# A two-layer diffusion block on one core: modulation rows loaded in half blocks and moved out of the second layer's FFN, FFN parts chosen by layer, input sums on VectorE

## The chip, the cores and the metric

One core of a Trainium2 chip runs the whole program. The metric is device time in microseconds for one execution.

## The reference

Two layers run over 128 prompt tokens and 512 sample tokens, width 1024, float32. Two condition vectors, one for the prompt and one for the sample, give each layer a modulation of 6 × 1024 values:

```python
mod = silu(cond) @ w_ada[l] + b_ada[l]
sh1, sc1, g1, sh2, sc2, g2 = split(mod, 6)
h = rmsnorm(x, norm1_g) * (1 + sc1) + sh1
x = x + g1 * mixers(h)               # retention, differential and latent attention, gated, projected
h = rmsnorm(x, norm2_g) * (1 + sc2) + sh2
a, b = split(h @ w_ffn_in, 2)        # 1024 -> 2 x 2816
x = x + g2 * ((silu(a) * b) @ w_ffn_out)
```

After both layers a last RMSNorm gives the outputs; the mixers also return their caches.

## The kernel before

**Layout.** Activations lie transposed: 128 channels on the partitions, the 640 tokens along the free axis in two halves of 320. Each float32 product is made of three matmuls of `hi`/`lo` pairs, so every weight block is loaded as `raw`, cast by ScalarE to `whi` (L117), and VectorE subtracts to give `wlo` (L120). Layer 0 is called the first layer here, layer 1 the second.

**Modulation rows.** A layer's 6144 modulation values are 48 rows of 128 channels. `ada_rows` (L237) makes a row: POOL issues the load of a 128x1024 block `rawr` (L245), and VectorE multiplies it with each of the two conditions and sums into one column of `mod` (L248, two instructions a row, held in program order on VectorE). After the last row of a call it adds the bias to all rows of the call (L252). Rows 0 to 15 are sh1 and sc1, 16 to 23 g1, 24 to 39 sh2 and sc2, 40 to 47 g2.

**When rows are made.** `plan` gives each row a due point, `fill` is called at points in the stage, and rows that are due are issued there; what is left is issued by `flush`. Rows 16 to 39 are planned over the last branch and the output projection, which have 20 points; `norm2` for the first half flushes the rest. Rows 40 to 47 are planned at the very start of the layer's FFN (share 0 to 0.0277 of 72 points), with one `rawr` tile. In the first layer's FFN rows 0 to 15 of the second layer follow at shares 0.15 to 0.9.

**FFN** (`ffn`, L1217). The 22 blocks f of 128 hidden channels go through `up`: blocks 0 to NC-1 (NC = 5) in the plain form of 96 matmuls, the rest through `ffn_seven` (L1177), seven products and 84 matmuls, which needs sums of input quarters made by `ffn_forms` (L1120) from the eight `us` tiles. These sums run on POOL (L1130 to L1133). The results are the tiles `ghi`/`glo`, GB = 6 of each, which the `us` tiles share until the sums are made. The down projection goes in seven parts (FFN_PARTS): a part's eight units n each load weights (L1286) and for both halves multiply into a PSUM tile G or O and add the gated result to `x` (`x_add`, L1073). `x_add` reads g2, that is rows 40 to 47 with their bias. There are two such PSUM tiles, so a third down product waits for the first `x_add`. The units of a part are issued three after each `up` of the next part.

**Order.** The tile framework orders each engine's instructions by a timeline it works out when the program is built; only pinned instructions (the row products, and matmuls after block NC) keep their order in the program. Engines run their queues in order, so a VectorE instruction that waits for a load holds what is queued behind it.

Of the kernel before, what the change touches and what calls it, by code (L numbers as in the profile page):

```python
# [12 lines left out]
F32 = mybir.dt.float32  # L13
# [8 lines left out]
P = 128  # L22
# [15 lines left out]
FFN_PARTS = ((0, 3), (3, 6), (6, 9), (9, 12), (12, 15), (15, 18), (18, 22))  # L38
GB = 6
NC = 5  # L40
# [10 lines left out]
class Kern:  # L51
# [185 lines left out]
    def ada_rows(self, l, b0, b1, pool, raws, bufs):  # L237

        d = self.dve
        if l not in self.mod:  # L240
            self.mod[l] = self.const.tile([P, 48, 2], F32, name=f"mod{l}")
        mod = self.mod[l]
        for n in range(b0, b1):
            raw = raws.tile([P, 1024], F32, tag="rawr", name="rawr", bufs=bufs)
            self.pool.dma_start(out=raw, in_=self.io["w_adat"][l, n])  # L245
            junk = pool.tile([P, 1024], mybir.dt.bfloat16, tag="junk", name="junk")
            for i in range(2):
                self.tc.keep_in_program_order(d.scalar_tensor_tensor(  # L248
                    junk, raw, 1.0, self.csr[:, i, :], op0=ALU.mult, op1=ALU.mult, accum_out=mod[:, n, i:i + 1]))
            if n == b1 - 1:  # L250
                b = self.pv[:, V_ADA + 48 * l + b0:V_ADA + 48 * l + b1]
                d.tensor_tensor(mod[:, b0:b1], mod[:, b0:b1], b.unsqueeze(2).to_broadcast([P, b1 - b0, 2]), op=ALU.add)  # L252
            yield 1
# [866 lines left out]
    def ffn_forms(self, pool, us):  # L1120
# [6 lines left out]
        for k in range(4):  # L1127
            p, q = us[k], us[4 + k]
            e = self.pool
# [87 lines left out]
    def ffn(self, l, act, x, pool, hook, a, b, mid, us=None):  # L1217
# [21 lines left out]
        def hold(f):  # L1239
            g[f] = (pool.tile([P, T], F32R, tag="ghi", name="ghi", bufs=GB), pool.tile([P, T], F32R, tag="glo", name="glo", bufs=GB))  # L1240
# [19 lines left out]
        def up(f):  # L1260
            if us is not None and f >= NC:
                W = self.ffn_weights(pool, io["w_ffn_in"][l, f])
                self.fill()
                if f == NC:
                    self.pin = True
                    self.sctx.close()
                    state["xf"] = ExitStack()
# [14 lines left out]
        for p, (f0, f1) in enumerate(FFN_PARTS):  # L1282
            nf, lastp = f1 - f0, p == len(FFN_PARTS) - 1

# [18 lines left out]
            for f in range(max(f0, 2), f1):  # L1303
                up(f)
                for _ in range(min(3, len(waiting))):
                    waiting.pop(0)()
# [30 lines left out]
    def run(self):  # L1337
# [3 lines left out]
        for l in range(DEPTH):  # L1341
# [41 lines left out]
            adctx, rctx = ExitStack(), ExitStack()  # L1383
            adp = self.sb("ada", 1, adctx, "right")
# [7 lines left out]
            self.plan(21, (chain(self.ada_rows(l, 16, 24, adp, rp, 3), self.ada_rows(l, 24, 40, adp, rp, 3)), 24))  # L1392
# [172 lines left out]
```

## Time and profile before

| | us |
|---|---|
| time, median of 3 runs | 2530.13 |
| lowest and highest of them | 2522.33, 2540.38 |
| the profiled execution's own time | 2530.01 |
| its span in the trace | 2528.2 |
| TensorE matmul busy | 2395.5 |
| VectorE busy | 1847.1 |
| ScalarE busy | 1087.3 |
| GpSimd (POOL) busy | 197.4 |

Times within the trace count from the start of the span. The first layer's FFN lies at about 786 to 1275, the second's at about 2032 to 2510. PE is TensorE, DVE VectorE, ACT ScalarE, SP the engine that issues weight loads.

### The profile page before, as it was taken

Reading aid. Unit: us, or ns where it says so; the run is one execution under the profiler, and the core shown is the slowest. Engines: PE = TensorE matmul, PEld = TensorE weight load, DVE = VectorE, ACT = ScalarE, POOL = GpSimd, SP = SyncE. Lnnn points to the kernel's source line nnn. Section 1 sums busy time; section 2 is a strip of 40 time slices with the busy share of each in tenths; the row PEclk is TensorE's granted clock in tenths of the full one; section 3 lists DMA queues with packets and bytes.
Section 4 is the critical chain, followed back from the end, with each engine's and each line's share of the span. In section 5 each row is a group of like instructions: output and inputs, shape, how many; then the busy total and the mean of one; then the engine's idle time right before and its main releaser. Section 6 shows DMA issues by size and latency. Waiting matters only on the chain.

```text
span 2528.2 us, 43126 instructions
## 1 busy us (share of the span) xinstructions
PE 2395.5 (95%) x16828; PEld 2323.7 (92%) x16828; DVE 1847.1 (73%) x4022; ACT 1087.3 (43%) x2260; POOL 197.4 (8%) x299
## 2 busy tenths in 40 slices
PE   8999999999999799999999999999999996999997
PEld 5999998999999799999999998999999996999997
DVE  5877686566798678888777867765668885777776
ACT  5656465422235233333375655553232352333333
POOL 0000210000112100000000012000001030000001
PEclk9999999999999899999999999999999998999999
DMA  6212322322651333333231123223135422222222
GB/s 259 76 56 70 97 88 65 108 78 77 204 188 52 110 100 111 102 100 101 74 123 56 58 76 115 73 63 127 59 142 176 151 68 83 85 87 76 79 78 67
DMA packets 83883, 250.02 MB, mean 99 GB/s; under 512 B 10880, under 2 KB 28512, under 8 KB 82656
## 3 DMA queue, kind: packets, MB, share of 16 engines
q1 hardware_dynamic: 56160, 164.13, 19.9%
q0 software_dynamic: 21472, 77.17, 9.4%
q10 hardware_dynamic: 6048, 5.98, 0.7%
q8 instruction: 132, 2.16, 0.4%
q14 instruction: 71, 0.58, 0.1%
HBM read 227.01 MB, written 20.22 MB: 98 GB/s over the span
## 4 chain that ended last, share of the span: by engine, by line
PE 79%; DVE 11%; DMA 3%; issue 3%; ACT 3%; DVEq 0%; ACTq 0%; POOLq 0%
PE G L133 32%; PE S L133 24%; PE Tp L133 6%; DVE x L1076 2%; DVE wlo L120 2%; PE O L866 1%; PE S L1116 1%; DMA rawr<-w_adat 1%; PE S L1115 1%; PE S L1114 1%; DMA raw<-w_ffn_in 1%; PE Tp L669 1%; DVE junk L248 1%; ACT whi L117 1%; DVE v L1213 1%
## 5 line engine op out<-in xcount | busy, mean ns | idle before, releaser
L117 ACT CAST whi<-raw 128x1024 fp32r<-128x1024 f32 (+3 forms) x362 | 299.9, 831 | 499.7 <-PE G L133 197.5
L120 DVE TENSOR_TENSOR wlo<-raw,whi 128x1024 fp32r<-128x1024 f32 (+3 forms) x362 | 346.2, 958 | 111.5 <-ACT whi L117 109.8
L133 PE MATMUL G<-whi,hhi 128*128 128x256 f32 x1040 | 299.1, 288 | 4.7 <-DVE rvs L819 2.9
L133 PE MATMUL G<-whi,hlo 128*128 128x256 f32 x1040 | 295.2, 284 | 0.0
L133 PE MATMUL G<-wlo,hhi 128*128 128x256 f32 x1040 | 294.5, 283 | 0.0
L133 PE MATMUL G<-ghi,whi 128*128 128x320 f32 x704 | 224.6, 320 | 51.7 <-DVE x L1076 50.6
L248 DVE SCALAR_TENSOR_TENSOR junk<-rawr,csr 128x1024 bf16<-128x1024 f32 x160 | 196.5, 1228 | 33.8 <-DMA rawr<-w_adat 32.6
L133 PE MATMUL G<-glo,whi 128*128 128x320 f32 x704 | 219.8, 312 | 0.6 <-DVE glo L120 0.6
L133 PE MATMUL G<-ghi,wlo 128*128 128x320 f32 x704 | 219.5, 312 | 0.0
L133 PE MATMUL S<-hhi,whi 128*128 128x320 f32 x648 | 204.4, 315 | 7.6 <-DVE gt L1043 7.4
L133 PEld LDWEIGHTS G<-whi,hhi 128*128 128x128 f32 x1040 | 198.0, 191 | 8.2 <-DVE rvs L819 3.8
L133 PE MATMUL S<-hhi,wlo 128*128 128x320 f32 x648 | 201.6, 311 | 0.0
L133 PE MATMUL S<-hlo,whi 128*128 128x320 f32 x648 | 201.5, 311 | 0.0
L133 PEld LDWEIGHTS G<-wlo,hhi 128*128 128x128 f32 x1040 | 198.4, 191 | 0.1
L133 PEld LDWEIGHTS G<-whi,hlo 128*128 128x128 f32 x1040 | 198.3, 191 | 0.0
L133 PEld LDWEIGHTS G<-ghi,whi 128*128 128x128 f32 x704 | 134.1, 191 | 65.7 <-issue 49.7
L1076 DVE SCALAR_TENSOR_TENSOR x<-G,mod,x 128x320 f32<-128x320 f32 (+2 forms) x384 | 156.4, 434 | 37.0 <-PE G L133 36.2
L133 PE MATMUL G<-hhi,whi 128*128 128x320 f32 x512 | 161.7, 316 | 7.3 <-DVE x L1076 4.1
L133 PE MATMUL G<-hlo,whi 128*128 128x320 f32 x512 | 158.9, 310 | 0.0
L133 PE MATMUL G<-hhi,wlo 128*128 128x320 f32 x512 | 158.8, 310 | 0.0
L459 DVE TENSOR_REDUCE mx<-S 128x1 f32<-128x640 f32 (+1 forms) x160 | 113.3, 714 | 50.4 <-PE S L837 29.2
L133 PEld LDWEIGHTS G<-glo,whi 128*128 128x128 f32 x704 | 134.4, 191 | 1.3 <-DVE glo L120 1.1
(435 smaller groups left out, 6653.9 us busy)
## 6 DMA issues: line engine op xcount, KB each, us to landing
raw<-w_ffn_in SPq DMA_DIRECT2D x88, 512.0 KB, 3.6
rawr<-w_adat POOLq DMA_DIRECT2D x80, 512.0 KB, 4.4
raw<-w_gate SPq DMA_DIRECT2D x48, 512.0 KB, 3.8
raw<-w_ffn_out SPq DMA_DIRECT2D x96, 192.0 KB, 2.4
raw<-w_diff SPq DMA_DIRECT2D x24, 512.0 KB, 3.9
raw<-w_branch SPq DMA_DIRECT2D x24, 512.0 KB, 3.6
raw<-w_ret SPq DMA_DIRECT2D x24, 512.0 KB, 3.9
raw<-w_ada SPq DMA_DIRECT2D x16, 512.0 KB, 9.7
```

Of the source, the lines that this page charges most:

```text
L117: (eng or self.act).copy(hi, src)
L120: (eng or self.dve).tensor_tensor(lo, src, hi.bitcast(F32), op=ALU.subtract)
L133: ins = self.pe.matmul(*args, **kw)
L248: self.tc.keep_in_program_order(d.scalar_tensor_tensor(junk, raw, 1.0, self.csr[:, i, :], op0=ALU.mult, op1=ALU.mult, accum_out=mod[:, n, ...
L459: self.dve.tensor_reduce(mx, sv, axis=AX.XY if len(sv.shape) == 3 else AX.X, op=ALU.max)
L669: self.pe.transpose(t[:, 256 * kb + 128 * i:256 * kb + 128 * i + 128], ps[i][:, 128 * (k0 + kb):128 * (k0 + kb) + 128], self.ident)
L866: pe.matmul(o[:, :128], at[:, 128 * kb:128 * kb + 128], V[:, kb0 + kb, :], start=kb == 0, stop=kb == nk - 1)
L1076: self.dve.scalar_tensor_tensor(x[h][:, n, c0:c1], ps[:, c0:c1], g[:, n, gi:gi + 1], x[h][:, n, c0:c1], op0=ALU.mult, op1=ALU.add)
L1114: self.pe.matmul(o, lh, rh, start=k == 0, stop=False)
L1115: self.pe.matmul(o, lh, rl, start=False, stop=False)
L1116: self.pe.matmul(o, ll, rh, start=False, stop=k == nk - 1)
L1213: d.scalar_tensor_tensor(ga, gb, -1.0, ga, op0=ALU.mult, op1=ALU.mult)
```

## The change

The layer indices are those of the code. Rows 40 to 43 of layer 0 are planned behind rows 16 to 39 in the branch stage (22 points instead of 21, shares 0.9 to 1.0); rows 44 to 47 stay at the start of layer 0's FFN. Rows 40 to 47 of layer 1 are made in layer 0's FFN, after rows 0 to 15 of layer 1, so that FFN now makes 4 + 24 rows and layer 1's FFN none. Rows made in the FFN are loaded as two 128x512 halves into two tiles; each half has its own two products, and a small addition joins the two halves' sums at the end of a call. In layer 1 the FFN has six parts, the seven-product form starts at block 4, there are seven `ghi`/`glo` tiles, and the pool with the conditions is closed before the input sums are placed. The input sums go to VectorE in both layers.

```diff
-FFN_PARTS = ((0, 3), (3, 6), (6, 9), (9, 12), (12, 15), (15, 18), (18, 22))
-GB = 6
-NC = 5
+FFN_PARTS = (((0, 3), (3, 6), (6, 9), (9, 12), (12, 15), (15, 18), (18, 22)), ((0, 4), (4, 8), (8, 12), (12, 15), (15, 18), (18, 22)))
+FFN_HELD = (6, 7)
+FFN_CLASSIC = (5, 4)
...
-    def ada_rows(self, l, b0, b1, pool, raws, bufs):
+    def ada_rows(self, l, b0, b1, pool, raws, cols, bufs):
...
+        part = self.const.tile([P, 48, 2], F32, tag="modp", name="modp", bufs=1) if cols < 1024 else None
         for n in range(b0, b1):
-            raw = raws.tile([P, 1024], F32, tag="rawr", name="rawr", bufs=bufs)
-            self.pool.dma_start(out=raw, in_=self.io["w_adat"][l, n])
...
+            for c in range(0, 1024, cols):
+                raw = raws.tile([P, cols], F32, tag="rawr", name="rawr", bufs=bufs)
+                self.pool.dma_start(out=raw, in_=self.io["w_adat"][l, n][:, c:c + cols])
+                junk = pool.tile([P, cols], mybir.dt.bfloat16, tag="junk", name="junk")
+                for i in range(2):
+                    self.tc.keep_in_program_order(d.scalar_tensor_tensor(
+                        junk, raw, 1.0, self.csr[:, i, c:c + cols], op0=ALU.mult, op1=ALU.mult,
+                        accum_out=(part if c else mod)[:, n, i:i + 1]))
             if n == b1 - 1:
...
+                if part is not None:
+                    d.tensor_tensor(mod[:, b0:b1], mod[:, b0:b1], part[:, b0:b1], op=ALU.add)
...
-            e = self.pool
+            e = self.dve
...
-            if us is not None and f >= NC:
+            if us is not None and f >= FFN_CLASSIC[l]:
...
                     self.sctx.close()
+                    if l == 1:
+                        self.adctx.close()
...
-                for _ in range(min(3, len(waiting))):
+                for _ in range(min(2 if lastp and nf < FFN_HELD[l] - 2 else 3, len(waiting))):
...
-            self.plan(21, (chain(self.ada_rows(l, 16, 24, adp, rp, 3), self.ada_rows(l, 24, 40, adp, rp, 3)), 24))
+            self.plan(22, (chain(self.ada_rows(l, 16, 24, adp, rp, 1024, 3), self.ada_rows(l, 24, 40, adp, rp, 1024, 3)), 24, 0.0, 0.9),
+                      *([(self.ada_rows(0, 40, 44, adp, rp, 1024, 3), 4, 0.9, 1.0)] if l == 0 else []))
...
-            own = (self.ada_rows(l, 40, 48, adp, fp, 1), 8, 0.0, 0.0277)
             if l == 0:
-                self.plan(72, own, (self.ada_rows(1, 0, 16, adp, fp, 1), 16, 0.15, 0.9))
+                self.plan(72, (self.ada_rows(0, 44, 48, adp, fp, 512, 2), 4, 0.0, 0.0277),
+                          (chain(self.ada_rows(1, 0, 16, adp, fp, 512, 2), self.ada_rows(1, 40, 48, adp, fp, 512, 2)), 24, 0.12, 0.9))
...
-                self.plan(72, own)
+                self.plan(0)
```

## Rows read from the trace of the kernel before

**Rows 1.** The page: busy time by engine, and the chain's shares by engine.

```profile
PE 2395.5 (95%) x16828; PEld 2323.7 (92%) x16828; DVE 1847.1 (73%) x4022; ACT 1087.3 (43%) x2260; POOL 197.4 (8%) x299
...
PE 79%; DVE 11%; DMA 3%; issue 3%; ACT 3%; DVEq 0%; ACTq 0%; POOLq 0%
```

**Rows 2.** Windows: stretch; length, busy us (instructions) by engine, PE clock, DMA, GB/s.

```profile
801.54:902.32 100.78, 79.46 (x495) 77.88 (x493) 69.86 (x109) 31.04 (x58) 25.32 (x24) 0.88 0.26 84
2047.94:2149.75 101.81, 79.28 (x495) 77.55 (x494) 69.84 (x109) 31.14 (x58) 24.77 (x23) 0.88 0.25 78
900.00:1250.00 350.00, 335.03 (x2231) 328.43 (x2231) 286.36 (x478) 120.29 (x182) 7.92 (x15) 1.00 0.32 99
2148.70:2498.70 350.00, 342.79 (x2293) 335.97 (x2292) 256.59 (x427) 123.66 (x190) 0.00 (x0) 1.00 0.25 77
...
870.00:880.00 10.00, 1.30 (x9) 1.03 (x8) 3.84 (x9) 1.72 (x4) 0.53 (x1) 0.73 0.49 158
880.00:890.00 10.00, 4.07 (x15) 4.10 (x16) 6.82 (x13) 1.04 (x1) 0.53 (x1) 0.50 0.18 52
```

**Rows 3.** The chain in order of time, first layer's FFN: start, us, what.

```profile
944.71 3.52 PE S L133 x24
```

**Rows 4.** PE timeline: waits at the start of both FFNs, with releaser in brackets.

```profile
818.14 0.42 PE L1116 MATMUL S<-hhi,wlo 128*128 128x320 f32 x1 [1.77 <-DVE wlo L120]
...
856.89 0.41 PE L1116 MATMUL S<-hhi,wlo 128*128 128x320 f32 x1 [3.95 <-DVE wlo L120]
...
885.93 0.61 PE L133 MATMUL G<-ghi,whi 128*128 128x320 f32 x1 [14.63 <-DVE x L1076]
...
2134.64 0.60 PE L133 MATMUL G<-ghi,whi 128*128 128x320 f32 x1 [14.91 <-DVE x L1076]
```

**Rows 5.** DVE timeline, first layer's FFN: first row product, the bias, the first addition.

```profile
819.82 1.88 DVE L248 SCALAR_TENSOR_TENSOR junk<-rawr,csr 128x1024 bf16<-128x1024 f32 x1
...
884.90 0.17 DVE L252 TENSOR_TENSOR mod<-mod,pv 128x16 f32<-128x16 f32 x1
885.11 1.14 DVE L1076 SCALAR_TENSOR_TENSOR x<-G,mod,x 128x128 f32<-128x128 f32 x3
```

**Rows 6.** Tile rawr, 760 to 900: VectorE's idle time until the load, and landing times.

```profile
  DMA rawr<-w_adat: 14.6, 6
...
DMA to landing us min/median/max: 3.7/4.1/5.9
```

**Rows 7.** DMA issues of the whole run: KB each, median us to landing.

```profile
rawr<-w_adat POOLq DMA_DIRECT2D x80, 512.0 KB, 4.4
...
V<-dproj POOLq DMA_DIRECT2D x8, 256.0 KB, 3.4
```

**Rows 8.** Groups by form on DVE: count, busy us, mean ns, idle before.

```profile
L248 DVE SCALAR_TENSOR_TENSOR junk<-rawr,csr 128x1024 bf16<-128x1024 f32 x160 | 196.5, 1228 | 33.8 <-DMA rawr<-w_adat 32.6
...
L1169 DVE SCALAR_TENSOR_TENSOR raw<-ts,raw 128x512 f32<-128x512 f32 x34 | 23.3, 685 | 0.1
```

**Rows 9.** DVE timeline at the first layer's flush, from the last planned row on.

```profile
776.12 1.22 DVE L248 SCALAR_TENSOR_TENSOR junk<-rawr,csr 128x1024 bf16<-128x1024 f32 x1
...
780.48 0.90 DVE L319 TENSOR_TENSOR nt<-x,nr 128x320 f32<-128x320 f32 x2
...
784.30 0.48 DVE L120 TENSOR_TENSOR hlo<-us,hhi 128x320 fp32r<-128x320 f32 x1
```

**Rows 10.** PE timeline, first product of the first layer's FFN.

```profile
788.80 0.42 PE L1115 MATMUL S<-hlo,whi 128*128 128x320 f32 x1 [0.16 <-DVE hlo L120]
```

**Rows 11.** Tile us, 795 to 830: ns min/median/max, first and last start.

```profile
L120 DVE TENSOR_TENSOR hlo<-us,hhi x10: 478/485/1171, 795.2 to 806.8; 128x320 fp32r<-128x320 f32 x10
...
L120 DVE TENSOR_TENSOR x5lo<-us,x5hi x4: 1165/1166/1168, 807.9 to 812.3; 128x320 fp32r<-128x320 f32 x4
...
L120 DVE TENSOR_TENSOR x67lo<-us,x67hi x4: 1497/1500/1503, 813.4 to 824.9; 128x640 fp32r<-128x640 f32 x4
L1133 POOL TENSOR_TENSOR us<-us x4: 1448/1663/1862, 815.6 to 824.2; 128x320 f32<-128x320 f32 x4
```

More of the change, by code (lines that the diff above doesn't have):

```diff
@@ L242, in ada_rows @@
         mod = self.mod[l]
+        part = self.const.tile([P, 48, 2], F32, tag="modp", name="modp", bufs=1) if cols < 1024 else None
         for n in range(b0, b1):
-            raw = raws.tile([P, 1024], F32, tag="rawr", name="rawr", bufs=bufs)
-            self.pool.dma_start(out=raw, in_=self.io["w_adat"][l, n])
[L246 to L249, printed above, removed]
+            for c in range(0, 1024, cols):
[6 more added lines that the diff above has]
+                        accum_out=(part if c else mod)[:, n, i:i + 1]))
             if n == b1 - 1:
                 b = self.pv[:, V_ADA + 48 * l + b0:V_ADA + 48 * l + b1]
+                if part is not None:
+                    d.tensor_tensor(mod[:, b0:b1], mod[:, b0:b1], part[:, b0:b1], op=ALU.add)
                 d.tensor_tensor(mod[:, b0:b1], mod[:, b0:b1], b.unsqueeze(2).to_broadcast([P, b1 - b0, 2]), op=ALU.add)
@@ L1239, in hold @@
         def hold(f):
-            g[f] = (pool.tile([P, T], F32R, tag="ghi", name="ghi", bufs=GB), pool.tile([P, T], F32R, tag="glo", name="glo", bufs=GB))
+            g[f] = (pool.tile([P, T], F32R, tag="ghi", name="ghi", bufs=FFN_HELD[l]), pool.tile([P, T], F32R, tag="glo", name="glo", bufs=FFN_HELD[l]))
         def load(f):
@@ L1260, in up @@
         def up(f):
-            if us is not None and f >= NC:
+            if us is not None and f >= FFN_CLASSIC[l]:
                 W = self.ffn_weights(pool, io["w_ffn_in"][l, f])
                 self.fill()
-                if f == NC:
+                if f == FFN_CLASSIC[l]:
                     self.pin = True
                     self.sctx.close()
+                    if l == 1:
+                        self.adctx.close()
                     state["xf"] = ExitStack()
@@ L1281, in ffn @@
         waiting = []
-        for p, (f0, f1) in enumerate(FFN_PARTS):
-            nf, lastp = f1 - f0, p == len(FFN_PARTS) - 1
+        for p, (f0, f1) in enumerate(FFN_PARTS[l]):
+            nf, lastp = f1 - f0, p == len(FFN_PARTS[l]) - 1
             def dload(n, p=p, f0=f0, nf=nf):
@@ L1383, in run @@
             adctx, rctx = ExitStack(), ExitStack()
+            self.adctx = adctx
             adp = self.sb("ada", 1, adctx, "right")
@@ L1398, in run @@
             fp = self.sb("ffn", 1, fctx)
-            us = [fp.tile([P, T], F32, tag=("ghi", "glo")[k % 2], name="us", bufs=GB) if k < 6 else
+            us = [fp.tile([P, T], F32, tag=("ghi", "glo")[k % 2], name="us", bufs=FFN_HELD[l]) if k < 6 else
                   fp.tile([P, T], F32, tag=("thi", "tlo")[k % 2], name="us", bufs=2) for k in range(KT)]
```

## The prediction

> **What bounds the kernel now.** I read the page first: TensorE is busy for 95% of the span and makes 79% of the chain that ended last, VectorE 11% [rows 1]. So an edit pays only where TensorE stands idle or slow, and VectorE matters where TensorE waits for it. A table of windows over the span then showed two stretches that stand out, the starts of the two FFNs, and those I cut out exactly. From the first plain product with both halves to the end of the first down products there are 495 matmuls in 100.78 us in the first layer and 495 in 101.81 us in the second [rows 2]. At full speed 24 such matmuls take 3.52 us, 0.1467 each [rows 3], so 495 need 72.6 us: the two starts lose 28.2 and 29.2 us.
>
> Who holds TensorE there? Its timeline names these waits in the first layer: 1.77 us at 818 (and a shorter one behind it) and 3.95 at 857 for `wlo`, 14.63 at 886 for an `x_add`; the second layer repeats them, with 14.91 in the last place [rows 4]. The rest of the loss is a low clock: the granted share was 0.73 and 0.50 in the two 10 us around the long wait [rows 2]. The `x_add` itself starts 0.2 us after the bias of rows 40 to 47 [rows 5]: TensorE waits for modulation rows. They are eight rows on one tile, each a cycle of issue, landing and two products, and VectorE sits idle for six of the loads, 14.6 us in all, as a load lands 4.1 us after its issue (median) [rows 6]; VectorE runs its queue in order, so the `wlo` behind a product waits too (the 3.95 us).
>
> **Second layer: no rows in its FFN.** The long wait, the 3.95 us and the low clock after them go. What stays is the wait for `wlo` at the second plain block, since its weight tiles come free only when the block before is done: the 1.77 us, the shorter wait and a slow stretch behind them, about 4 us. Gain 29.2 − 4 = 25 (bounds 20, if the first seven-product block brings a wait of its own, to 27). What would be late next is the weights for block 4, whose preparation VectorE does; it is busy for 256.6 of 350 us in this FFN [rows 2], so there is room.
>
> Block 4 in seven products: 84 matmuls instead of 96, 12 × 0.1467 = 1.8 us less. One part fewer: TensorE's gaps in this layer's steady stretch are 350 − 342.79 = 7.2 us [rows 2], of which one part in seven can give 1.0; I take 0.5. Closing the pool with the conditions early adds a dependence on its last reader, which is the last row product of the output projection, some 25 us before the sums: nothing.
>
> **First layer: four rows in halves at the start.** The loads shrink to 256 KB. No such load of rows exists before; the nearest rows are POOL's loads of `V`, 256 KB in 3.4 us, against 4.4 for 512 KB [rows 7]. A half's two products cost 2 × 0.685 us (the 128x512 instruction of the same kind) against 2 × 1.23 for a whole block [rows 8]. With two tiles, two halves pass in about 0.5 + 3.4 + 1.5 = 5.4 us. The first row is loaded ahead; three more take 16 us, so the bias comes about 25 us after the first product instead of 65 (819.82 to 884.90 [rows 5]), near 845. TensorE would reach its third down product at about 863 (885.93 − 14.63 = 871, where it stopped [rows 4], less 8 of shorter waits), so the addition is in time by some 18 us. Gain 28.2, less the same 4 that stay and 3 for an order built for quicker loads: 21 (bounds 8 to 25).
>
> The rule that speaks against this: the Trainium skill (DMA: Bandwidth & Descriptors, section Anatomy of one DMA — SWDGE (gpsimd) path) gives a POOL-issued transfer a fixed cost near 2.0 us plus its bytes at 436 GB/s. A block in two transfers then pays 2.0 us more; the rows above agree in direction (two times 3.4 is 2.4 more than 4.4). What it would do if the two did not overlap is the last rival.
>
> **First layer: rows 40 to 43 before the norm.** Planned from 0.9 × 22 on, the first is due at point 20.1, and the stage has 20 points: all four fall to the flush in front of the second norm. Before, one row was there, from 776.12 on; `nt` followed at 780.48 and the first `hlo` at 784.30 [rows 9], and TensorE at 788.8 waited 0.16 us for an `hlo` [rows 10], so nothing covers a delay there. Three more rows are 6 × 1.22 = 7.3 us of VectorE. Between two products VectorE's order lets another ready instruction pass (the timeline has `x_add` there), so part of the norm goes on: +5 us taken, bounds 0 (the norm passes them) and 8 (all of it, and a dip of the clock). In the second layer row 39 is no longer left for the flush, 2 × 1.22 = 2.4 us off the same place: −1 (0 to −2.4). The denser rows in the branch stage, 24 over 19.8 points instead of 21, fall where TensorE hardly waits: nothing.
>
> **First layer: 24 rows beside the FFN instead of 16.** In 350 us the first layer's steady stretch starts 2231 matmuls, the second's 2293, and the first has 16 rows of products in it [rows 2]: 62 × 0.1467 = 9.1 us, 0.57 a row. 24 rows at that price cost 13.7, and a half-block row has 4 × 0.685 = 2.74 us of products instead of 2.46, which makes 15: +5 to +6; shorter instructions hold an `x_add` less long. I take +5; bounds −2 (what stalls is the large transfer beside a weight load) and +26 (all the added VectorE work, 24 × 2.74 − 16 × 2.46, reaches TensorE).
>
> **Input sums on VectorE.** POOL's last four sums take 1.4 to 1.9 us each, with the chain's end near 826, and meanwhile VectorE's own instructions are slower: `x5lo` 1.166 us where the same shape takes 0.485, `x67lo` 1.50 [rows 11]. Some 13 instructions at 0.68 us more are 9 us given back; 16 sums at 0.485 add 7.8 (bounds −9 to +8 on VectorE, in each layer). The `wlo` that TensorE waits 1.77 us for is one of the slowed ones; I leave that inside the 4 us that stay.
>
> **Sum.** −25 − 1.8 − 0.5 − 1 in the second layer, −21 + 5 + 5 in the first: −39.3 us. The profiled execution took 2530.01 us for its span of 2528.2, and the median of the three runs is 2530.13, so no correction between them: 2530.0 − 39.3 = 2490.7, said as 2490.
>
> **Rivals.**
> 1. Better than that: the norm passes the four rows, 24 rows cost no more than 16 did, and the first layer's start gains 24. 2490 − 5 − 5 − 3 = 2477. For it: VectorE is idle for 27% of the span [rows 1], so slots are there. Against: row products are pinned in program order. Chance 0.13.
> 2. The addition still comes late in the first layer: the order of TensorE's queue was built for loads that are quicker than they land (2.4 us of wait in each of six loads [rows 6]); eight halves at that price are 19 us, which eats the 18 in hand and stalls the queue piecemeal, so the start gains only 8. 2490 + 13 = 2503. Chance 0.10.
> 3. VectorE becomes the bound of the first layer's FFN: 286.4 + 26.4 = 313 of 350 us busy, and it already waits in order for loads and casts between. The whole +26 in place of +5: 2511. Against it: 37 of 350 us would still be free. Chance 0.10.
> 4. Slower: the halves of a row don't overlap, and each of the 24 rows in the first layer's FFN waits for two landings in turn, 2 × 3.4 − 4.4 = 2.4 us more than a whole block, on VectorE's queue with all that is behind. 24 × 2.4 = 58 in place of +5: 2543. It turns the sign from 41/2.4, 17 rows, on. By the skill's page named above it would be 2.0 us a row, 48 us, an estimate: 2533. Against it: the two tiles hold both halves, and a tile is refilled long before its next use: a row comes every 350/24 = 15 us, a load lands in about 4. Chance 0.05.
>
> The forecast has the remaining 0.62, and alone runs from 2477 to 2505.
>
> **Range and chances.** All low bounds together give about 2470, all high ones about 2530. Rival 1 lies inside from 2472 up, rivals 2 and 3 up to 2513; beyond are rival 4 and the ends of the others, under 2 in 10. A measurement here can tell about 1% from no change, so faster means under 2504.8: nearly all of the forecast (0.60), rival 1 (0.13) and half of rival 2 (0.05), 0.78. Within 1%: rival 3, the rest of 2, the forecast's tail and some of rival 4 (2543 is 0.5% above), 0.18. Slower: 0.04.
>
> **What would show it.** Right: in the second layer no TensorE wait for `x_add` over 1 us before the first seven-product block, and 495 matmuls from the start take about 77 us; in the first layer the bias some 25 us after the first half's product and no wait near 14 us; a new wait for `hlo` of 3 to 8 us at the first product of the first FFN; VectorE near 313 us in that layer's 350. Wrong: `x5lo` still at 1.17 us without POOL's sums; the first layer's steady stretch losing over 15 us against the second's; idle time for half blocks over 20 us in all; or the long wait back under another name, such as `ts` waiting for weights.

## The result, and the profile after

The changed kernel took 2489.69 us (median of 4 runs, 2487.97 to 2492.84), the kernel before 2526.23 (4 runs beside them, 2518.21 to 2540.38): a ratio of 0.9851, 95% interval 0.9803 to 0.9898. The prediction was 2490, faster: 39.3 us less. The medians differ by 36.5. The profiled executions, which the rest of this document reads, differ by 42.4: a span of 2485.8 (time 2487.97, the lowest of its four runs) against 2528.2 before. The page of the profile after, busy time by engine and the loads of modulation rows (KB each, median us to landing), for [rows 1, 7]:

```profile
PE 2383.3 (96%) x16816; PEld 2315.5 (93%) x16816; DVE 1840.8 (74%) x4146; ACT 1092.2 (44%) x2259; POOL 170.9 (7%) x295
...
rawr<-w_adat POOLq DMA_DIRECT2D x52, 512.0 KB, 4.2
...
rawr<-w_adat POOLq DMA_DIRECT2D x56, 256.0 KB, 3.3
```

Shares of the whole span say little here; stretches do. I cut each FFN at landmarks that both kernels have: the first matmul on `nss` (the second norm's sum), the first and the last matmul on `x67` (the seven-product form), the last down product. "Start" runs from the first landmark to the second, "steady" to the third, "end" to the last. The loss of a stretch is its length less 0.1467 us for each matmul that starts in it [rows 3] (2127 in the first steady stretch; the window below counts 2129, with those that reach into it), which prices idle time and a low clock together and does not care how the work was divided. Windows of the kernel after: both starts, both steady stretches, and 350 us of the first FFN as in [rows 2]:

```profile
778.30:887.40 109.10, 100.31 (x658) 97.87 (x657) 89.14 (x200) 48.41 (x93) 5.38 (x10) 0.98 0.28 86
2014.60:2086.90 72.30, 69.48 (x454) 67.89 (x453) 55.58 (x113) 42.08 (x81) 0.00 (x0) 0.98 0.19 60
887.40:1231.10 343.70, 322.16 (x2129) 316.56 (x2129) 296.35 (x583) 114.15 (x172) 24.19 (x45) 0.99 0.35 110
2086.90:2428.40 341.50, 338.00 (x2281) 334.23 (x2280) 249.89 (x392) 120.25 (x177) 0.00 (x0) 1.00 0.26 80
900.00:1250.00 350.00, 327.43 (x2162) 321.31 (x2161) 297.78 (x591) 116.69 (x178) 23.65 (x44) 0.99 0.34 108
```

The same two steady stretches of the kernel before (the first FFN at 905.8, the second at 2153.3):

```profile
905.80:1239.00 333.20, 319.32 (x2129) 313.48 (x2128) 276.73 (x460) 114.56 (x172) 7.92 (x15) 0.99 0.32 100
...
2153.30:2477.40 324.10, 317.98 (x2128) 311.92 (x2128) 241.09 (x394) 113.83 (x172) 0.00 (x0) 1.00 0.25 79
```

The first steady stretch has the same matmuls in both kernels and became 10.5 us longer: TensorE's busy time grew by 2.8 us and its idle time by 7.7 (343.70 − 322.16 against 333.20 − 319.32). That is the one place where the change costs. In all, by the landmarks:

| us | before | after | predicted change | measured |
|---|---|---|---|---|
| first FFN, loss of the start | 31.1 | 13.0 | −21 + 5 | −18.1 |
| first FFN, loss of the steady stretch | 21.3 | 31.8 | +5 | +10.5 |
| second FFN, loss of the start | 32.1 | 6.1 | −25 − 1 | −26.0 |
| second FFN, loss of the rest | 14.3 | 7.9 | −0.5 | −6.4 |
| second FFN, 12 matmuls fewer | | | −1.8 | −1.8 |
| all outside the two FFNs | | | 0 | −0.6 |
| sum | | | −39.3 | −42.4 |

The waits that were named before the change are gone or small. TensorE's timeline after, for [rows 4, 10]: the start of the first FFN, and further down the two longest waits of the steady stretch:

```profile
787.82 0.41 PE L1121 MATMUL S<-hlo,whi 128*128 128x320 f32 x1 [1.25 <-DVE hlo L121]
...
794.81 0.81 PE L291 MATMUL Tp<-nss,ct 128*128 128x320 f32 x2 [2.76 <-DVE nss L283]
...
823.77 0.56 PE L1122 MATMUL S<-hhi,wlo 128*128 128x320 f32 x2 [1.69 <-DVE wlo L121]
826.04 0.41 PE L1122 MATMUL S<-hhi,wlo 128*128 128x320 f32 x1 [1.13 <-DVE wlo L121]
...
1004.40 0.60 PE L134 MATMUL G<-ghi,whi 128*128 128x320 f32 x1 [2.37 <-DVE x L1082]
...
1048.59 0.50 PE L134 MATMUL G<-ghi,whi 128*128 128x320 f32 x1 [3.77 <-DVE x L1082]
```

There is no wait of 14 us any more, and the wait for `wlo` at the second plain block (1.77 before) stays at 1.69, as the prediction left it. New is the delay at the second norm: 1.25 us for `hlo` and 2.76 for the norm's sum `nss`, whose VectorE part stands behind a row product:

```profile
793.11 1.24 DVE L251 SCALAR_TENSOR_TENSOR junk<-rawr,csr 128x1024 bf16<-128x1024 f32 x1
...
794.25 0.51 DVE L283 TENSOR_TENSOR nss<-nss,nsq 128x320 f32<-128x320 f32 x1
```

VectorE's timeline after, first row product and the join and bias of the four rows, for [rows 5]:

```profile
825.89 0.69 DVE L251 SCALAR_TENSOR_TENSOR junk<-rawr,csr 128x512 bf16<-128x512 f32 x1
...
849.77 0.16 DVE L257 TENSOR_TENSOR mod<-mod,modp 128x8 f32<-128x8 f32 x1
849.96 0.17 DVE L258 TENSOR_TENSOR mod<-mod,pv 128x8 f32<-128x8 f32 x1
```

The bias comes 24 us after the first product in place of 65 [rows 5], and the third down product starts at 855.9 without a wait. And the contention that POOL's sums made is gone; the tiles `x5lo` and `x67lo` after (ns min/median/max), for [rows 11]:

```profile
L121 DVE TENSOR_TENSOR x5lo<-us,x5hi x8: 486/490/498, 814.3 to 2050.2; 128x320 fp32r<-128x320 f32 x8
...
L121 DVE TENSOR_TENSOR x67lo<-us,x67hi x8: 821/826/837, 815.1 to 2056.8; 128x640 fp32r<-128x640 f32 x8
```

### The profile page after: what moved, and what is told of

It reads as the page before. It is cut to its first block, busy times and chain, and to the rows that moved or that the text cites. A ratio compares the mean times of both kernels' runs of the same rounds, so it can differ in the third digit from the quotient of the medians.

```text
span 2485.8 us, 43255 instructions
## 1 busy us (share of the span) xinstructions
PE 2383.3 (96%) x16816; PEld 2315.5 (93%) x16816; DVE 1840.8 (74%) x4146; ACT 1092.2 (44%) x2259; POOL 170.9 (7%) x295
## 4 chain that ended last, share of the span: by engine, by line
PE 73%; issue 11%; DVE 9%; DMA 4%; ACT 3%; POOL 0%; DVEq 0%; POOLq 0%; ACTq 0%
PE G L134 32%; PE S L134 22%; PE Tp L134 4%; DMA rawr<-w_adat 2%; PE O L872 2%; PE S L1122 1%; PE Tp L675 1%; PE S L1121 1%; PE S L1120 1%; DVE wlo L121 1%; DVE junk L251 1%; DVE x L1082 1%; PE O L650 1%; DMA raw<-w_ffn_in 1%; PE O L649 1%
## 5 line engine op out<-in xcount | busy, mean ns | idle before, releaser
L134 PE MATMUL G<-ghi,whi 128*128 128x320 f32 x704 | 223.3, 317 | 26.5 <-DVE x L1082 23.5
L251 DVE SCALAR_TENSOR_TENSOR junk<-rawr,csr 128x512 bf16<-128x512 f32 (+1 forms) x216 | 204.1, 945 | 16.0 <-DMA rawr<-w_adat 14.3
L1082 DVE SCALAR_TENSOR_TENSOR x<-G,mod,x 128x128 f32<-128x128 f32 (+2 forms) x360 | 147.3, 436 | 38.2 <-PE G L134 37.2
```

Of the source, the lines that this page charges most:

```text
L134: ins = self.pe.matmul(*args, **kw)
L251: self.tc.keep_in_program_order(d.scalar_tensor_tensor(junk, raw, 1.0, self.csr[:, i, c:c + cols], op0=ALU.mult, op1=ALU.mult, accum_out=( ...
L1082: self.dve.scalar_tensor_tensor(x[h][:, n, c0:c1], ps[:, c0:c1], g[:, n, gi:gi + 1], x[h][:, n, c0:c1], op0=ALU.mult, op1=ALU.add)
```

## The experiments

All kernels by the same landmarks; the loss in us of each stretch (the rest of the second FFN is its steady stretch and its end):

| kernel | start 1 | steady 1 | start 2 | rest 2 | span |
|---|---|---|---|---|---|
| before | 31.1 | 21.3 | 32.1 | 14.3 | 2528.2 |
| before, sums on VectorE alone | 23.1 | 19.5 | 24.8 | 14.3 | 2508.9 |
| changed | 13.0 | 31.8 | 6.1 | 7.9 | 2485.8 |
| changed, sums on POOL | 19.5 | 30.8 | 6.3 | 8.2 | 2491.7 |
| changed, old parts in layer 2 | 14.3 | 28.9 | 7.2 | 15.5 | 2497.5 |
| changed, whole blocks | 15.5 | 31.4 | 6.1 | 7.9 | 2494.0 |
| changed, eight rows at the start | 12.2 | 33.5 | 6.1 | 7.7 | 2495.5 |
| changed, transfers of 22 rows left out | 14.4 | 17.3 | 6.1 | 7.7 | 2480.3 |
| changed, products of 24 rows cut | 15.7 | 16.7 | 6.2 | 7.9 | 2482.1 |
| changed, rows placed by halves | 14.3 | 23.5 | 4.6 | 8.2 | 2482.5 |
| changed, fill call in the tail | 10.0 | 30.0 | 4.6 | 7.7 | 2478.9 |
| fill call in the tail, six parts in both FFNs | 8.9 | 15.2 | 4.6 | 7.8 | 2468.5 |
| fill call in the tail, six parts, rows placed by halves | 7.3 | 19.3 | 6.1 | 7.7 | 2471.0 |

How far may these be read? Where an edit doesn't reach, the rest of the second FFN repeats within 0.5 us (7.7 to 8.2). The other stretches scatter more: the start of the first FFN is 13.0 to 15.7 in four kernels that have the same code there (changed, old parts, transfers left out, products cut), its steady stretch 28.9 to 33.5 in five (changed, sums on POOL, old parts, eight rows, fill call in the tail), the start of the second 4.6 to 6.3. In the first start it is mostly the clock. At the second plain block TensorE waits 1.69 and 1.13 us for `wlo` in the changed kernel and 1.74 and 1.13 in the one with the products cut, but the granted clock stayed at 1.00 in the one and fell in the other, from 48 matmuls in the 10 us to 36:

```profile
820.00:830.00 10.00, 7.18 (x48) 6.66 (x47) 10.00 (x17) 5.85 (x8) 0.54 (x1) 1.00 0.31 92
```

```profile
824.00:834.00 10.00, 7.14 (x36) 6.61 (x35) 10.00 (x17) 5.85 (x8) 0.54 (x1) 0.78 0.29 92
```

So a difference under 3 us in the first start, or under 5 in its steady stretch, says nothing by itself. What lies outside the FFNs varies more: from the first FFN's last down product to the second's first `nss` the kernels with one and the same code there took 746 to 753 us, and the first `nss` came at 778 to 783. The kernel before, run again beside the groups of experiments, had medians from 2521.80 to 2531.63. So a single span is good to some 5 us at best, and verdicts below go by stretches. The changed kernel, the one with the fill call in the tail and the two built on that were run four times each, and have medians.

**Sums back on POOL.**

```diff
-            e = self.dve
+            e = self.pool
```

> The changed kernel with the input sums back on POOL. Loss means the length of a stretch less 0.1467 us for each matmul in it. The forecast's step says the sums are worth about nothing on VectorE (9 us of slowed instructions against 7.8 us of added ones), hidden but for the wait for wlo: both FFN starts (4.5 and 4.0 us of loss in the changed kernel, from the two first blocks' second half to the first seven-product block) get 0.5 to 1.5 us worse each, x5lo is back at 1.17 us, the time rises by 1 to 3 us. Rival: POOL's chain is what the first seven-product block waits for now that nothing else holds TensorE; then the second layer's start loses 5 us or more.

Measured: 2493.95 us. The second start doesn't change (6.3 against 6.1), so the rival fell; the first loses 19.5, 6.5 more than the changed kernel and 4 to 6.5 more than the kernels with the same code there, which is more than I expected. TensorE's timeline there (kernel with the sums on POOL):

```profile
825.41 0.42 PE L1120 MATMUL S<-hhi,whi 128*128 128x320 f32 x1 [2.97 <-ACT whi L118]
827.60 0.90 PE L1122 MATMUL S<-hhi,wlo 128*128 128x320 f32 x2 [1.34 <-DVE wlo L121]
830.83 0.64 PE L1122 MATMUL S<-hhi,wlo 128*128 128x320 f32 x1 [0.85 <-DVE wlo L121]
```

A weight block comes late there, and the clock falls behind it. In the second layer, where VectorE has no rows to make, the same slower instructions cost nothing: what the sums are worth depends on what else VectorE carries.

**Sums alone, on the kernel before.** The same line in the kernel before, nothing else.

> The kernel before with the input sums on VectorE alone. Theory: the start of each FFN there is set by the bias of rows 40 to 47, and POOL's sums lie beside that wait, so the 6.4 us that POOL's sums cost in the changed kernel's first start do not come back here: 0 to -3 us, 2527 to 2530. Rival, the slowed VectorE instructions delay the row products that lead to the bias: -6 us in each layer, about 2518.

Measured: 2510.99 us, 18 below the kernel before: a loss of 8.0 us less in the first start and 7.3 in the second, and 1.7 in the first steady stretch. The three stretches give 17.0. My expectation was wrong and the rival's mechanism right, at a larger size. TensorE still waits 15.26 us for the addition, but all of it happens earlier: the first FFN began 2.2 us later than before, and yet the bias came 4.8 us earlier than [rows 5] has it, 7.0 earlier counted from the FFN's start. VectorE's timeline of that kernel, and TensorE's:

```profile
878.82 1.22 DVE L248 SCALAR_TENSOR_TENSOR junk<-rawr,csr 128x1024 bf16<-128x1024 f32 x1
...
880.08 0.18 DVE L252 TENSOR_TENSOR mod<-mod,pv 128x16 f32<-128x16 f32 x1
```

```profile
881.11 0.61 PE L133 MATMUL G<-ghi,whi 128*128 128x320 f32 x1 [15.26 <-DVE x L1076]
```

**Old parts in the second layer.** FFN_PARTS, FFN_HELD and FFN_CLASSIC of layer 1 as they were (seven parts, 6, 5).

```diff
-FFN_PARTS = (((0, 3), (3, 6), (6, 9), (9, 12), (12, 15), (15, 18), (18, 22)), ((0, 4), (4, 8), (8, 12), (12, 15), (15, 18), (18, 22)))
-FFN_HELD = (6, 7)
-FFN_CLASSIC = (5, 4)
+FFN_PARTS = (((0, 3), (3, 6), (6, 9), (9, 12), (12, 15), (15, 18), (18, 22)),) * 2
+FFN_HELD = (6, 6)
+FFN_CLASSIC = (5, 5)
```

> The changed kernel with the FFN parts, the held tiles and the first seven-product block of the second layer as before. The forecast's terms: 1.8 us for the block and 0.5 us for the part less, so the time rises by about 2 us. Rival, from the two traces: the second layer's steady stretch lost 12.3 us before and 7.3 after, its tail 2.0 and 0.5, because a part of four blocks keeps each PSUM tile busy for 12 matmuls instead of 9 and the addition no longer holds the next; then the second layer's FFN alone rises by 7 to 9 us and the first layer's stays.

Measured: 2499.32 us; the second FFN is 10.4 us longer than in the changed kernel, 1.8 for the 12 matmuls and 8.7 in losses, of which 7.6 lie behind its start. The window of its steady stretch:

```profile
2122.00:2447.30 325.30, 317.95 (x2128) 311.87 (x2127) 241.24 (x394) 113.94 (x172) 0.00 (x0) 1.00 0.25 78
```

and TensorE's waits in it (us in total, times, longest):

```profile
PE G L134 <- DVE x L1082: 7.0, 21, 1.3
```

In the changed kernel the same wait is 2.4 us in 7. VectorE's load hardly differs (241 of 325 us, 250 of 341), so it isn't the load. The place of the waits is telling. After an `up` three units follow, each with two down products, one for each half. All 21 waits stand at the third or the fifth of these six products, where a PSUM tile is wanted whose addition is not done. In a part of three blocks a down product is 9 matmuls, so the addition has the 18 matmuls of the first two, 2.6 us at 0.1467; in a part of four it has 24, 3.5 us. That is the rival's mechanism.

**Whole blocks, one tile.**

```diff
-                self.plan(72, (self.ada_rows(0, 44, 48, adp, fp, 512, 2), 4, 0.0, 0.0277),
-                          (chain(self.ada_rows(1, 0, 16, adp, fp, 512, 2), self.ada_rows(1, 40, 48, adp, fp, 512, 2)), 24, 0.12, 0.9))
+                self.plan(72, (self.ada_rows(0, 44, 48, adp, fp, 1024, 1), 4, 0.0, 0.0277),
+                          (chain(self.ada_rows(1, 0, 16, adp, fp, 1024, 1), self.ada_rows(1, 40, 48, adp, fp, 1024, 1)), 24, 0.12, 0.9))
```

> The changed kernel, but rows made in the first layer's FFN come as whole 128x1024 blocks with one tile. If halves and two tiles matter at the start: the bias of rows 44 to 47 comes 8 us a row after the first, near 858 instead of 850, and the start's loss rises from 4.5 to 7 or more. If they matter beside the FFN: the steady stretch, 31.7 us of loss with halves, changes; by products alone (2 x 1.23 us a row instead of 4 x 0.685) it should fall by some 3 us, by transfers (one of 512 KB instead of two of 256 KB) it could rise by up to 5. Rival: the halves do nothing in either place, both losses within 1.5 us.

Measured: 2495.76 us, but by stretches the halves are worth 2.5 us in the first start, no more than kernels with the same code differ by there, and 0.4 the other way in the steady stretch, where VectorE now waits for a block 7 times, 10.2 us in all. The bias came near 858 as expected, and four whole rows are in time too: VectorE's timeline of this kernel has the bias at 857.55, and the third down product starts at 861.3 without a wait. So the rival stands: the halves with their second tile do nothing that can be told from the scatter, in either place.

```profile
857.55 0.16 DVE L258 TENSOR_TENSOR mod<-mod,pv 128x8 f32<-128x8 f32 x1
```

**Eight rows in halves at the start.** Rows 40 to 43 go back from the place before the norm to the FFN.

```diff
-            self.plan(22, (chain(self.ada_rows(l, 16, 24, adp, rp, 1024, 3), self.ada_rows(l, 24, 40, adp, rp, 1024, 3)), 24, 0.0, 0.9),
-                      *([(self.ada_rows(0, 40, 44, adp, rp, 1024, 3), 4, 0.9, 1.0)] if l == 0 else []))
+            self.plan(22, (chain(self.ada_rows(l, 16, 24, adp, rp, 1024, 3), self.ada_rows(l, 24, 40, adp, rp, 1024, 3)), 24, 0.0, 0.9))
...
-                self.plan(72, (self.ada_rows(0, 44, 48, adp, fp, 512, 2), 4, 0.0, 0.0277),
+                self.plan(72, (self.ada_rows(0, 40, 48, adp, fp, 512, 2), 8, 0.0, 0.0277),
```

> The changed kernel with all eight rows 40 to 47 of layer 1 in half blocks at the start of its FFN, none in front of the second norm. It tells the half blocks from the smaller number of rows. From the first row product to the bias the changed kernel took 24 us for four rows, 6 a row. Theory, the start is cured by four rows fewer: eight take about 48 us, the bias comes near 870 where TensorE's third down product wants it near 852, so a wait for x_add of 10 to 18 us is back, less 4 for the flush that goes: loss from the first nss to the first matmul on x67 20 to 27 in place of 13.0, span 2492 to 2500. Rival, the halves on two tiles are what cured it: no wait over 3 us there, loss near 9, span near 2482.

Measured: 2497.31 us. That lies in the range of my theory by luck: of the 9.7 us of span more than the changed kernel, 4.0 lie before the FFN and 4.9 between the FFNs, where the variation is. The first start lost 12.2 against 13.0, and here it has no rows in front of the norm to pay for. The bias came at 868.78 as worked out (46 us for eight rows), yet the long wait did not come back.

```profile
868.78 0.17 DVE L258 TENSOR_TENSOR mod<-mod,pv 128x16 f32<-128x16 f32 x1
```

The reason is the order of TensorE's queue: here, as in the kernel before, a whole plain block, 96 matmuls, stands between the second and the third down product, which starts at 871.7 without a wait; in the changed kernel that product stands ahead of nearly all of the block. So my theory fell. With the sums on VectorE, either change is enough for the first start, eight rows in halves or four rows whole; eight rows whole are not (the sums alone, above).

**The fill call in the output projection's tail.** Before, the tail of the output projection issued no planned rows, so all four of the change fell to the flush in front of the norm. Here each of the last four weight loads calls `fill`.

```diff
         def load(n):
             wu[n] = self.load_w(self.io["w_out"][l, n], 1024)
+            self.fill()

         for n in range(SKEW):
             load(n)
-            self.fill()
```

> The changed kernel with a point for due rows at each weight load of the output projection's tail, so rows 40 to 43 of the first layer are issued there instead of at the flush before the second norm. Theory: those rows, six instructions more than before of 1.22 us in front of the norm, cost the first plain block 5.3 us (loss 1.3 before, 6.6 after), and VectorE has idle time in the tail: the loss falls back to 1 to 3 us and the time by 4 to 5 us. Rival: in the tail they hold the additions there, and TensorE loses the same 5 us a few microseconds earlier.

Measured: 2482.55 us (median of 4, 2480.66 to 2491.1), ratio to before 0.9824, interval 0.9803 to 0.9845. The wait for `nss` and the slow clock behind it are gone from the second norm; 1.36 us for `hlo` stay, and a `wlo` some 30 us later is now followed by the lower clock (0.67 from 820 to 830), as in others of the table. The windows of 10 us there, first of the changed kernel:

```profile
785.00:795.00 10.00, 5.80 (x36) 5.01 (x35) 10.00 (x23) 3.17 (x6) 0.00 (x0) 1.00 0.35 105
795.00:805.00 10.00, 10.00 (x57) 9.84 (x57) 9.87 (x28) 7.03 (x16) 0.00 (x0) 0.83 0.01 2
```

And of the kernel with the fill call in the tail:

```profile
785.00:795.00 10.00, 8.64 (x56) 7.95 (x56) 10.00 (x28) 6.96 (x16) 0.00 (x0) 1.00 0.31 103
795.00:805.00 10.00, 10.00 (x70) 10.00 (x69) 8.57 (x22) 9.00 (x18) 0.00 (x0) 1.00 0.00 0
```

With TensorE idle for 4.2 of 10 us the granted clock was 0.83 in the next 10, 57 matmuls in place of 70. The loss from the first `nss` matmul to the fourth fell from 6.9 to 2.9: the flush cost 4 us there, of which the idle time and the clock each carry a part. Over the whole start 3.0 are left of it.

**Transfers or products?** Two kernels for the steady stretch of the first FFN, where the price was wrong. In the first only blocks 0 and 40 of layer 2 are loaded there:

```diff
-                raw = raws.tile([P, cols], F32, tag="rawr", name="rawr", bufs=bufs)
-                self.pool.dma_start(out=raw, in_=self.io["w_adat"][l, n][:, c:c + cols])
+                if l == 0 or cols == 1024 or n in (0, 40):
+                    raw = raws.tile([P, cols], F32, tag="rawr", name="rawr", bufs=bufs)
+                    self.pool.dma_start(out=raw, in_=self.io["w_adat"][l, n][:, c:c + cols])
```

> The 24 rows of layer 2 in the first FFN multiply halves that were loaded only for blocks 0 and 40: 22 of the 24 rows' transfers are left out, their products stay (so most of these modulation rows hold other values). In the changed kernel TensorE loses 31.7 us from the first to the last matmul on x67 in the first layer (343.7 us for 2127 matmuls at 0.1467). Theory, the products on VectorE hold the x_add: the loss stays at 27 to 32 and the span within 5 us of 2485.8. Rival, the landings or the contention of the transfers do it: it falls to about 13, which the second layer lost with the same seven parts and no rows, and the span is near 2468.

In the second the loads stay and the products shrink:

```diff
+            w = 16 if cols == 512 and l == 1 else cols
...
-                        junk, raw, 1.0, self.csr[:, i, c:c + cols], op0=ALU.mult, op1=ALU.mult,
+                        junk[:, :w], raw[:, :w], 1.0, self.csr[:, i, c:c + w], op0=ALU.mult, op1=ALU.mult,
```

> The same 24 rows keep all their transfers, and their products take 16 columns in place of 512 (the rest of each product is left out). Theory, the products on VectorE: the loss of that stretch falls from 31.7 to 13 to 18 us, the span to about 2470. Rival, the transfers: it stays at 27 to 32, the span near 2485. Both together, with a product that waits for its landing as the carrier: 20 to 25.

Measured: 2482.14 and 2483.88 us, the loss of the stretch 17.3 and 16.7. Each alone takes away 14 to 15 us (the second layer's stretch of the kernel before, with the same parts and no rows, lost 12.2), so neither the transfers nor the work on VectorE explains the 31.8 by itself, and no theory that I had written down gives both numbers. The windows of the stretch, without the transfers and with the short products:

```profile
890.80:1220.00 329.20, 317.96 (x2129) 311.89 (x2128) 298.17 (x591) 114.22 (x173) 1.08 (x2) 1.00 0.27 81
...
892.20:1220.90 328.70, 318.09 (x2129) 312.03 (x2128) 252.00 (x584) 114.44 (x172) 24.06 (x45) 1.00 0.36 116
```

and TensorE's waits for an `x_add` in the first of them:

```profile
PE G L134 <- DVE x L1083: 10.1, 21, 1.3
```

VectorE is busy for 298 of 329 us here, 91%, more than in the changed kernel (296 of 344, 86%), and TensorE loses less. So VectorE's busy share was not the bound. Nor did the transfers slow the weight loads: the blocks of `w_ffn_in` land in 3.7 us (median) with them and in 3.9 without. What needs both is a product that stands in VectorE's queue and waits for its landing. The changed kernel's trace shows three such waits, 7.8 us in all; one of them, on POOL's timeline:

```profile
988.84 0.54 POOL L248 DMA_DIRECT2D rawr<-w_adat  x1 [7.97 <-DVE junk L251]
991.10 0.54 POOL L248 DMA_DIRECT2D rawr<-w_adat  x1 [1.72 <-DVE junk L251]
```

and on VectorE's:

```profile
994.47 0.69 DVE L251 SCALAR_TENSOR_TENSOR junk<-rawr,csr 128x512 bf16<-128x512 f32 x1 [2.82 <-DMA rawr<-w_adat]
...
996.43 1.22 DVE L1172 TENSOR_TENSOR ts<-raw 128x1024 f32<-128x1024 f32 x1
...
1002.45 1.22 DVE L121 TENSOR_TENSOR wlo<-raw,whi 128x1024 fp32r<-128x1024 f32 x1
1003.58 0.67 DVE L1082 SCALAR_TENSOR_TENSOR x<-G,mod,x 128x128 f32<-128x128 f32 x2
```

Two rows are due close together: the second row's half is issued at 988.84, when the first row's product gives its tile back, and lands some 5 us later. Its product waits 2.82 us, `ts` and the rest of the weights for the next block stand behind it, and the `x_add` behind those starts at 1003.58: TensorE's 2.37 us at 1004.40, shown above. VectorE is never idle from 994.47 on, and four row products stand in front of this addition, 2.5 us of its queue. So 2.82 us of waiting and 2.5 of products lie ahead of a wait of 2.37: here either one, taken away, would be enough, which fits that each kernel loses so little. VectorE's waits of 2.75 and 2.22 us at 1125.32 and 1188.58 are followed, ten us later each, by TensorE waits of 2.30 and 1.93. The longest TensorE wait (3.77 at 1048.59) follows another one, of 3.38 us for a weight block of `w_ffn_in`, again with four row products in front of the addition. One caution: leaving the loads out also moves some row products forward in the order that the framework works out, so this run is not the changed kernel with the waits alone removed.

**Rows placed by halves.** To take away the close pairs and keep all loads and products, the generator stops after each half.

```diff
+                if c + cols < 1024:
+                    yield 1
...
-                self.plan(72, (self.ada_rows(0, 44, 48, adp, fp, 512, 2), 4, 0.0, 0.0277),
-                          (chain(self.ada_rows(1, 0, 16, adp, fp, 512, 2), self.ada_rows(1, 40, 48, adp, fp, 512, 2)), 24, 0.12, 0.9))
+                self.plan(72, (self.ada_rows(0, 44, 48, adp, fp, 512, 2), 8, 0.0, 0.0277),
+                          (chain(self.ada_rows(1, 0, 16, adp, fp, 512, 2), self.ada_rows(1, 40, 48, adp, fp, 512, 2)), 48, 0.12, 0.9))
```

> The changed kernel, whose row generator stops after each half block: the plan places 48 halves over the first FFN (and 8 at its start) where it placed 24 (and 4) whole rows. Loads and products are the same. Theory, what costs is two rows on each other's heels: the second row's half is issued when its tile comes free, lands 3 to 5 us later, and the product that waits for it holds the weight preparation and with it the x_add. Then VectorE's three waits for half blocks (7.8 us) fall under 2 us and TensorE's loss from the first to the last matmul on x67 from 31.7 to 15 to 20, with the span near 2472. Rival, the sum of VectorE's work, which stays the same: 28 to 32, span near 2486.

Measured: 2484.30 us; VectorE no longer waits for a half block in the steady stretch, and the loss there falls from 31.8 to 23.5. Its window:

```profile
888.10:1223.60 335.50, 320.70 (x2130) 315.10 (x2129) 297.86 (x587) 113.94 (x172) 24.46 (x46) 0.99 0.36 113
```

and TensorE's waits:

```profile
PE G L134 <- DVE x L1084: 14.6, 21, 1.8
```

That lies between the two forecasts: the close pairs were about 8 us of it (5 to 10, by the scatter of that stretch). The 6 to 7 us that are left above the two runs before, each of which leaves out the transfers or most of the products, no run here takes apart. Spread out like this, 24 rows cost 23.5 − 12.2 = 11.3 us over the stretch without rows, 0.47 a row, where 16 rows in the kernel before cost 9.1, 0.57 a row.

**Six parts in the first FFN too.** On top of the fill call in the tail (the plan's points go from 72 to 64, since there are fewer units):

```diff
-FFN_PARTS = (((0, 3), (3, 6), (6, 9), (9, 12), (12, 15), (15, 18), (18, 22)), ((0, 4), (4, 8), (8, 12), (12, 15), (15, 18), (18, 22)))
+FFN_PARTS = (((0, 3), (3, 7), (7, 11), (11, 15), (15, 18), (18, 22)), ((0, 4), (4, 8), (8, 12), (12, 15), (15, 18), (18, 22)))
...
-                self.plan(72, (self.ada_rows(0, 44, 48, adp, fp, 512, 2), 4, 0.0, 0.0277),
-                          (chain(self.ada_rows(1, 0, 16, adp, fp, 512, 2), self.ada_rows(1, 40, 48, adp, fp, 512, 2)), 24, 0.12, 0.9))
+                self.plan(64, (self.ada_rows(0, 44, 48, adp, fp, 512, 2), 4, 0.0, 0.0312),
+                          (chain(self.ada_rows(1, 0, 16, adp, fp, 512, 2), self.ada_rows(1, 40, 48, adp, fp, 512, 2)), 24, 0.135, 0.9))
```

> The changed kernel with the fill call in the output projection's tail and with six parts in the first layer's FFN too: (0,3), (3,7), (7,11), (11,15), (15,18), (18,22), the plan's points 64 in place of 72. In the second layer six parts for seven saved 8.6 us of gaps. Theory, the gaps come at the parts' ends: 3 to 6 us less than with the tail's fill call alone (2482.6), 2477 to 2480. Rival, VectorE's row products set the waits here and the number of parts does not matter: 2481 to 2484. Slower: held blocks come free too late with four in a part and six places: 2487 or more.

Measured: 2469.99 us (median of 4, 2462.62 to 2470.3), ratio to before 0.9757, interval 0.9735 to 0.9778; the steady stretch loses 15.2 in place of 30.0. That is the best version of the study, below both kernels, and 12.6 us below the fill call in the tail, where I expected 3 to 6. Its window:

```profile
883.30:1210.40 327.10, 316.81 (x2129) 313.49 (x2129) 286.62 (x553) 112.03 (x164) 24.18 (x45) 0.99 0.37 115
```

and TensorE's waits for an `x_add`:

```profile
PE G L134 <- DVE x L1082: 10.2, 12, 2.0
```

VectorE still waits 6.4 us in 4 for half blocks here, so such a wait has no fixed price. In the parts of four blocks TensorE's waits stand at the third down product again, which now leaves the addition 24 matmuls in place of 18; that this room takes up the waits is how I read it, and no run shows it apart from the lighter load. With six parts the first layer has 8 units fewer, and VectorE's work in the stretch falls by 10 us (296.9 to 286.6).

**Six parts and halves together.** The last kernel with the rows placed by halves, as above (8 and 48).

> The kernel with the fill call in the tail and six parts in both FFNs (2470.0), with the rows placed by halves. Theory: its four waits for half blocks (6.4 us) go and the loss of the steady stretch falls from 15.2 to 10 to 13: 2465 to 2468. Rival: with six parts the waits had slack behind them, so nothing changes: 2469 to 2471. Slower: a half at nearly every point leaves no point of VectorE's queue free of a product: 2473 or more.

Measured: 2473.18 us (median of 4, 2472.77 to 2475.35), ratio 0.9775, interval 0.9754 to 0.9796: not better, and the steady stretch loses 19.3. VectorE waited 14.4 us in 5 for half blocks, more than without the halves' placing, so it is no cure in itself: the order of the queue came out such that products again stand ahead of their landings. At equal parts more of that wait went with more loss (7.8 and 31.8 against none and 23.5; 14.4 and 19.3 against 6.4 and 15.2), but the second pair differs by no more than the scatter of that stretch.

## Why the prediction was right, and where it was not

- **Second layer's start, −25 and −1: right.** No wait for `x_add` before the first seven-product block; the loss fell by 26.0, and by 25.8 with the sums still on POOL, so the rows that leave are enough for it.
- **First layer's start, −21 and +5: right in sum (−18.1), wrong in its reason.** The step "the loads shrink to 256 KB ... two halves pass in about 5.4 us" put the whole gain down to the halves and the smaller number of rows; 24 us for four rows is that pace. But the sums on VectorE carry 4 to 6.5 of the gain, and with them there four whole rows gained 15.6 of the 18.1, eight in halves, with nothing in front of the norm, 18.9: one of the two was enough, and the halves beside the four rows were worth nothing that can be told from the scatter. The +5 for the flush is right in size: removing it gave 4 at the norm. The wait of 3 to 8 us for `hlo` that was to show it came as 1.25 for `hlo` and 2.76 for `nss`.
- **The sums, taken as nothing: mis-sized.** "I leave that inside the 4 us that stay" priced the instructions of VectorE that POOL slows, and only against the waits that remain after the change. Alone in the kernel before the sums' move gives 17 us by stretches, two fifths of the 42.4, since there the rows and the weights both queue behind the slowed instructions. In the changed kernel 4 to 6.5 are left, all in the first layer. The prediction's total hardly suffered, because the rows that leave the start cure the same delay.
- **Rows beside the first FFN, +5: half of the real +10.5.** The step "0.57 a row" is the term that failed: an average over 16 rows spread out, taken as the price of 24 that come partly in pairs. With the halves spread out it held (0.47 a row, +2.2 for the stretch in place of +10.5); about 8 us more came from rows close together, where a product waits for its landing with the weights and the addition behind it. That this needs the wait and the products both is argued from one such place and fits the two runs that take one of them out; 6 to 7 us stay open. The price depends on the parts too, for with six of them 24 rows fit into a stretch that loses 15.2, less than the 21.3 of 16 rows before. The sign that the prediction set for itself, over 15 us more loss than in the second layer's steady stretch, did show: 31.8 against 7.3.
- **One part fewer, −0.5: the real −6.4.** I divided TensorE's gaps by seven parts, as if each part had its own. They stand at the third and fifth down product behind each `up`, and a longer part leaves the addition more time there. The old parts in the second layer bring 7.6 of loss back behind the start. Whether the parts, the seventh tile or the earlier seven-product form does it was not separated there; in the first FFN the parts, with their plan, gave 14.8.
- **The two errors cancel, which is luck.** +5.5 and −5.9 meet, and the sum is right to about 3 us, whether by the medians (−36.5) or by the profiled executions (−42.4), with two of its terms off by more than 5.
- **The rivals.** The norm did not pass the four rows and the 24 rows cost more than the 16 (rival 1). The addition was not late (rival 2). VectorE was not the bound (rival 3): 297.8 of 350 us, where I had worked out 313. Rival 4's turning point is 44.3/2.4, 18 rows, since its price stands in place of the 5; I wrote 17, which changes nothing else. The halves do overlap (rival 4): a load of 256 KB lands in 3.3 us (median) and a half passes in about 3 on two tiles. The rule of the Trainium skill that stood beside it (DMA: Bandwidth & Descriptors, section Anatomy of one DMA — SWDGE (gpsimd) path) would give 2.6 us for 256 KB and 3.2 for 512, an estimate; the rows have 3.3 and 4.2. So a half block costs well over half of a whole one, as the rule has it, and on two tiles a row in halves still took 6 us; no run separates the halves from the second tile.

## What to carry to other kernels

Price a load on an engine that runs its queue in order by where it stands, not by its sum: ask of each product whether its data has landed when its turn comes, and what is queued behind it. Two cures of one wait don't add up: the sums were worth 17 us alone and 4 to 6.5 beside the others, so measure a part of a change both alone and taken out of the whole. And where TensorE waits for an addition to give a PSUM tile back, look at how long the products into each tile last: longer parts give the addition more time, and here they went with a larger gain (14.8 us) than spreading the load on the engine that adds (about 8). Last, compare kernels that have the same code in a stretch before you read a difference there: here they differ by 3 to 5 us.

## What the runs showed of the hardware

- POOL's elementwise sums slow VectorE's (1.166 us for `x5lo` with them, 0.49 without) whether or not that is on the path: in the kernel before it cost 8.0 and 7.3 us in the two starts, in the changed kernel 4 to 6.5 in the first and nothing in the second.
- After TensorE had been idle for 4.2 of 10 us, its granted clock was 0.83 in the next 10; the kernel that avoided the idle time kept 1.00 there. After shorter waits it is not settled by their length: with 1.69 and 1.13 us of waits the clock stayed at 1.00 in one kernel, with 1.74 and 1.13 at the same place it fell to 0.78 in another.
- A half of the bytes took 3.3 us against 4.2: 0.9 us saved for 256 KB.
